# Up projection: product 2 of neighbouring pairs as seven half-size products, and gate sums by an adding DMA

## Chip, cores and metric

The kernel runs on one core of one Trainium2 chip. The metric is the device time of one execution in microseconds (us), as the median of three runs. A profiled execution, recorded by the hardware profiler, is shown beside it.

PE is the matrix engine (TensorE), PEld its weight loads, DVE the vector engine, ACT the scalar engine, POOL the general-purpose engine that also issues DMAs, SP the engine that only issues DMAs. Each engine works through its own queue in order.

## What is computed

Two layers of a hybrid encoder over 1040 frames (16 learned meta frames and 1024 others) of width 1024 in float32. Each layer has attention (not touched here) and a gated feed-forward part:

```python
def conv_ffn(x, w_up, conv_w, conv_b, w_down):
    h = x @ w_up                      # 1024 -> 2 * 2816
    L = h.shape[1]
    hp = jnp.pad(h, ((0, 0), (CONV_W - 1, 0), (0, 0)))
    hc = conv_b
    for j in range(CONV_W):           # causal, width 3
        hc = hc + hp[:, j:j + L] * conv_w[j]
    u, g = jnp.split(hc, 2, axis=-1)
    return (jax.nn.silu(g) * u) @ w_down
```

The change is in `x @ w_up`.

## The kernel before

**Precision.** Every float32 operand is split into two parts, hi (rounded to the matrix engine's format) and lo (the rest). A product is three matmuls: w_hi x_hi, w_lo x_hi and w_hi x_lo (`mm3`, lines 222 to 224). For weights, `up_split` (lines 1067 to 1074) does the split: ACT casts hi (L1072), DVE subtracts to get lo (L1073), both over 128x512 elements (4 k-tiles of 128x128).

**Tiling.** The 5632 output columns are 22 *pairs*: pair j has 128 columns of u and the 128 columns of g that gate them. Channels lie on the 128 partitions, frames along the free dimension, cut into two halves of 520 (layer 0) or 516 and 516 (layer 1), t0 and t1. Within a half, matmuls run over 260 or 258 frames, into two PSUM banks.

**Seven products per pair.** A pair is a 2x2 block product: the block rows are u and g, the inner blocks are channels 0 to 511 and 512 to 1023 (4 k-tiles each), the block columns are the two halves of the frames. It is done in the form of Strassen and Winograd, with seven products p = 1 to 7 instead of eight. The weights are A11, A12 (u, low and high channels), A21, A22 (g) and sums of them: S1 = A21 + A22 (product 5), S2 = S1 - A11 (product 6), A11 - A21 (product 7), A12 - S2 (product 3). Products 1, 2 and 4 use A11, A12 and A22 as they are. The seven moving operands `X[1]` to `X[7]`, each split into hi and lo, are built once per layer (`make_t2` and so on) and stay in SBUF. Product 2 is A12 times `X[2]`, and it goes only into u's half t0.

One product is 4 k-tiles x 2 banks x 3 matmuls = 24 matmuls.

**Order.** `seq` is the order of (pair, product). From pair 5 on it is, for pair j: 2, 6, 5, 7, then product 1 of pair j + 1, then 4, 3. PE's order is fixed by this list; the order of the other engines' queues is laid down by a scheduler when the kernel is built. `ensure(i)` prepares weight operands up to four places ahead (`AHEAD`). hi and lo have three buffers for the even places and three for the odd ones.

**Where weights come from.** `block_operand` (lines 1037 to 1065) loads A11, A21, A22, A12 of a pair by four DMAs from SP when the pair's first product asks for them (L1045), and forms the sums on DVE (`combine`, L1055). A11 and A12 lie in a ring of 4 tiles (tag `raw`), the others in a ring of 7 (`raw2`). For the first five pairs (`N_DMA_SUM`) S1 is not formed on DVE: a DMA loads A21 into a tile (L1048) and a second DMA, from POOL, adds A22 onto it (L1049).

**PSUM.** Four places of two banks each: p0 and p1 alternate by pair for products 1, 6, 7, 4, which add onto one another (bank name a); p2 takes product 5 and then 3 (x); p3 takes product 2 (y, from pair 5 on).

**After each product** (`evacuate`, from line 1260): ACT copies the place of 1, 6, 7, 4 into hu or hg (L1264), DVE adds the others on top (L1263). After product 3 a pair is complete: `conv` (ACT L1252, DVE L1256 twice) for u and for g, SiLU (ACT L1283), the product (DVE L1287), and a store to memory from POOL (L1288).

**Slots.** 33 tiles of 128x1040 float32, and 6 more during the feed-forward part, are lent by `Slots` in the order in which they were given back. The seven moving operands take 4 each, 28 in all. hu, hg and the two results of `conv` take the rest in turn.

**The end of the up projection.** `prepare` is a generator that loads finished pairs back and builds the operands of the down projection, step by step (L337, L1381); `pump` lets it go on when slots are free. `during_last` calls it after each product of the last pair (21), as the moving operands are given back one after another. The down projection then runs first three pairs plainly (288 matmuls), then pairs 3 to 10 as block products, and so on.

## Time and profile before

| | |
|---|---|
| median of 3 runs | 2515.2 us (2514.78 to 2515.3) |
| profiled execution | 2518.04 us, its span 2516.3 us |
| granted clock of PE | 0.996 |
| PE, PEld | 2477.9 us (98%), 2383.8 us (95%), 18442 instructions each |
| DVE | 1767.2 us (70%), 3523 instructions |
| ACT | 1272.9 us (51%), 2733 instructions |
| POOL | 385.3 us (15%), 567 instructions |
| HBM | 177.29 MB read, 67.81 MB written |

The span runs from the first to the last instruction. In layer 0 the up projection lies at about 570 to 1014 us. A row of the timeline reads: start, duration, engine, line, operation, output <- inputs, shapes, count; in brackets, how long the engine was idle before it and what ended that. In a row of the groups by line, the numbers after the bar are busy time in us and the mean of one in ns, then idle time before them and what ended it. Matmul durations overlap; the pace of PE is read from start to start.

### The profile page before, as it was taken

What the parts mean: (1) busy time and instruction counts of PE and PEld (TensorE: products, weight loads), DVE (VectorE), ACT (ScalarE), POOL (GpSimd) and SP (SyncE); (2) the same over time, 40 slices, a digit from 0 to 9 for tenths busy, and PEclk for the clock granted to TensorE, in tenths of its full rate; (3) what the DMA queues carried; (4) which work ended last, traced back from release to release, by engine and by line L of the source; (5) the groups of instructions that cost most, each with busy time, mean ns of one, the idle gap of its engine ahead of it and who ended that gap; (6) DMA issues with size and microseconds to landing.
All of it is one profiled execution on the core that took longest, in us unless ns stands there. A gap on an engine that the chain in (4) does not pass through costs nothing.

```text
span 2516.3 us, 47049 instructions
## 1 busy us (share of the span) xinstructions
PE 2477.9 (98%) x18442; PEld 2383.8 (95%) x18442; DVE 1767.2 (70%) x3523; ACT 1272.9 (51%) x2733; POOL 385.3 (15%) x567
## 2 busy tenths in 40 slices
PE   9999999999999999999999999999999999999998
PEld 8999999999999999999999899999999999997786
DVE  8656777769877777853666666777798777787535
ACT  7346666636544445631443566665464444455312
POOL 2023433210000000100211234331100000001002
PEclk9999999999999999999999999999999999999999
DMA  3232134343322224763312222143433222258722
GB/s 133 67 88 74 44 92 133 118 130 97 119 81 81 77 77 146 193 170 106 107 57 69 74 80 78 58 153 109 142 105 101 76 79 78 80 166 186 194 56 74
DMA packets 118542, 260.94 MB, mean 104 GB/s; under 512 B 14880, under 2 KB 32544, under 8 KB 118320
## 3 DMA queue, kind: packets, MB, share of 16 engines
q1 hardware_dynamic: 93984, 182.79, 23.5%
q0 software_dynamic: 22464, 72.84, 10.4%
q8 instruction: 144, 2.36, 0.4%
q10 hardware_dynamic: 1872, 2.31, 0.3%
q14 instruction: 78, 0.64, 0.1%
HBM read 177.29 MB, written 67.81 MB: 97 GB/s over the span
## 4 chain that ended last, share of the span: by engine, by line
PE 81%; DVE 10%; ACT 4%; DMA 2%; issue 2%; SPq 0%; POOL 0%; DVEq 0%; ACTq 0%; POOLq 0%
PE up L222 11%; PE up L224 11%; PE up L223 11%; PE mm L222 7%; PE mm L224 7%; PE mm L223 7%; PE down L222 5%; PE down L223 5%; PE down L224 5%; PE av L720 3%; PE tr L694 2%; DVE S L661 1%; PE S L658 1%; ACT P L673 1%; PE S L659 1%
## 5 line engine op out<-in xcount | busy, mean ns | idle before, releaser
L222 PE MATMUL up<-x,hi 128*128 128x260 f32 (+1 forms) x2464 | 696.6, 283 | 0.0
L224 PE MATMUL up<-x,hi 128*128 128x260 f32 (+1 forms) x2464 | 695.9, 282 | 0.7 <-DVE x L1097 0.7
L223 PE MATMUL up<-x,lo 128*128 128x260 f32 (+1 forms) x2464 | 696.3, 283 | 0.0
L224 PEld LDWEIGHTS up<-x,hi 128*128 128x128 f32 x2464 | 465.3, 189 | 1.1 <-DVE x L1097 1.1
L222 PEld LDWEIGHTS up<-x,hi 128*128 128x128 f32 x2464 | 464.5, 189 | 0.4 <-DVE hu L1263 0.2
L223 PEld LDWEIGHTS up<-x,lo 128*128 128x128 f32 x2464 | 464.5, 189 | 0.1
L1073 DVE TENSOR_TENSOR lo<-raw,hi 128x512 fp32r<-128x512 f32 x364 | 247.7, 685 | 173.0 <-ACT hi L1072 172.7
L222 PE MATMUL mm<-xh,hi 128*128 128x348 f32 (+4 forms) x1056 | 362.7, 343 | 0.0
L224 PE MATMUL mm<-xl,hi 128*128 128x348 f32 (+4 forms) x1056 | 339.8, 322 | 0.0
L223 PE MATMUL mm<-xh,lo 128*128 128x348 f32 (+4 forms) x1056 | 339.4, 321 | 0.0
L1072 ACT CAST hi<-raw 128x512 fp32r<-128x512 f32 x364 | 223.6, 620 | 128.1 <-PE up L224 84.5
L222 PEld LDWEIGHTS mm<-xh,hi 128*128 128x128 f32 x1056 | 199.5, 189 | 5.2 <-issue 4.6
L223 PEld LDWEIGHTS mm<-xh,lo 128*128 128x128 f32 x1056 | 199.5, 189 | 0.7 <-issue 0.7
L224 PEld LDWEIGHTS mm<-xl,hi 128*128 128x128 f32 x1056 | 198.3, 188 | 0.4 <-issue 0.3
L189 ACT CAST hi<-raw 128x512 fp32r<-128x512 f32 (+2 forms) x168 | 97.4, 581 | 176.0 <-PE down L224 97.0
L223 PE MATMUL down<-ah,lo 128*128 128x260 f32 (+1 forms) x528 | 168.6, 319 | 0.4 <-DVE lo L191 0.3
L224 PE MATMUL down<-al,hi 128*128 128x260 f32 (+1 forms) x528 | 168.5, 319 | 0.0
L222 PE MATMUL down<-ah,hi 128*128 128x260 f32 (+1 forms) x528 | 168.2, 319 | 0.0
L673 ACT ACTIVATE P<-S,m 116x460 f32<-116x460 f32 (+2 forms) x224 | 124.8, 561 | 71.2 <-DVE m L661 67.6
L337 DVE TENSOR_TENSOR PT<-tr,PT 116x464 fp32r<-116x464 f32 (+3 forms) x240 | 122.8, 514 | 46.9 <-ACT PT L336 45.3
L1055 DVE TENSOR_TENSOR raw<-raw,raw 128x512 f32<-128x512 f32 x198 | 129.4, 684 | 17.2 <-DMA raw<-in_wd_dram 16.5
L1288 POOL DMA_DIRECT2D actd<-cv x44 | 23.6, 535 | 756.9 <-DVE cv L1287 735.9
(289 smaller groups left out, 5623.8 us busy)
## 6 DMA issues: line engine op xcount, KB each, us to landing
raw<-in_wm_dram SPq DMA_DIRECT2D x330, 256.0 KB, 2.7
raw<-in_wd_dram SPq DMA_DIRECT2D x64, 256.0 KB, 3.6
actd<-cv POOLq DMA_DIRECT2D x22, 520.0 KB, 3.0
actd<-cv POOLq DMA_DIRECT2D x22, 512.0 KB, 2.9
cb<-cd SPq DMA_DIRECT2D x16, 520.0 KB, 4.1
st<-actd SPq DMA_DIRECT2D x14, 520.0 KB, 4.9
st<-actd SPq DMA_DIRECT2D x14, 512.0 KB, 4.6
kA<-kA SPq DMA_DIRECT2D x24, 260.0 KB, 3.9
```

Of the source, the lines that this page charges most:

```text
L189: nc.scalar.copy(hi[:, :n, :], raw[:, :n, :])
L222: nc.tensor.matmul(ps, wh, xh[:, c0:c0 + n], start=first, stop=False, skip_group_check=more)
L223: nc.tensor.matmul(ps, wl, xh[:, c0:c0 + n], start=False, stop=False, skip_group_check=more)
L224: nc.tensor.matmul(ps, wh, xl[:, c0:c0 + n], start=False, stop=last, skip_group_check=more)
L337: nc.vector.tensor_tensor(out=lo, in0=src, in1=hi.bitcast(F32), op=ALU.subtract)
L658: nc.tensor.matmul(S[:rows, :n], q["qA"][e][:, qs], q["kA"][e][:, c0:k1], start=True, stop=False)
L673: nc.scalar.activation(P[:rows, :n], S[:rows, :n], AF.Exp, scale=-1.0, bias=m[:rows, nch - 1:nch], accum_out=(den if nch == 1 else d3[:row ...
L694: nc.tensor.transpose(tr[:w, 3 - j, :rows], P[:rows, o:o + w], id_)
L720: nc.tensor.matmul(av[:, a:b], w.rearrange("p a b -> p (a b)"), x, start=(t == ts[0] and part == 0 and i == 0), stop=(t == last and i == 1))
L1055: nc.vector.tensor_tensor(out=q[out][:, :nk, :], in0=q[a][:, :nk, :], in1=q[b][:, :nk, :], op=op)
L1072: nc.scalar.copy(hi[:, :nk, :], src[:, :nk, :])
L1073: nc.vector.tensor_tensor(out=lo[:, :nk, :], in0=src[:, :nk, :], in1=hi[:, :nk, :].bitcast(F32), op=ALU.subtract)
```

## The change

Three things.

1. **Pairs 6 to 21, two by two.** Product 2 of pair j and of pair j + 1 (j = 6, 8, ... 20) together are a block product again: the block rows are the two pairs, the inner blocks are the first two and the last two of the four k-tiles, the block columns are the two groups of 260 (258) frames of `X[2]`. They are done as seven half-size products m = 1 to 7, listed in `seq` as (j, SUB + m). Each has 2 k-tiles x 1 bank x 3 matmuls = 6 matmuls. Their weights are made by `sub_operand` from A12 of both pairs; their moving operands are views of `X[2]` for m = 1, 2, 3 and four new tiles `Y[4]` to `Y[7]` (one slot each), built by `second_level` in steps during pairs 4 and 5: two sums (`whole`) of hi and lo of `X[2]`, then for each Y one combination and one split (`make`). Their results go to place p3, one bank for 1, 6, 7, 4 and one for 2, then 5, 3; after each, DVE adds a bank onto a quarter of hu of one of the two pairs (`sub_evacuate`; m = 5 waits until product 1 of pair j + 1 was copied).
2. **S1 by DMA for all pairs.** The DMA that loads A21 and the adding DMA from POOL, for pairs 0 to 4 before, are used for all 22.
3. Product 3's weights A12 - S2 are written over S2, no longer over A12, which the half-size products still need. `X[2]` and `Y` are given back after the last half-size product of pair 20, with a call of `during_last`, and no longer after product 2 of pair 21.

```diff
-N_DMA_SUM = 5
+FIRST_SUB = 6
+SUB = 20
...
@@ up_operand
+        src = lambda j: (self.wm[lyr, M_UP + 2 * j], self.wm[lyr, M_UP + 2 * j + 1], 4, j)
+        if p > SUB:
+            self.block_raws(*src(j), fw, raws, True)
+            self.block_raws(*src(j + 1), fw, raws, only="A12")
+            return self.sub_operand(raws[j], raws[j + 1], p - SUB, fw, odd)
+        return self.block_operand(*src(j), p, fw, raws, odd, True)
+
+    def sub_operand(self, q, r, m, fw, odd):
+        A, B = q["A12"], r["A12"]
+        lo, hi = slice(0, 2), slice(2, 4)
+        tt = lambda out, a, b, op: self.nc.vector.tensor_tensor(out=out, in0=a, in1=b, op=op)
+        if m == 6:
+            q["s"] = fw.tile([128, 4, 128], F32, tag="raw2", name="raw2")
+            tt(q["s"][:, lo, :], B[:, lo, :], B[:, hi, :], ALU.add)
+            tt(q["s"][:, hi, :], q["s"][:, lo, :], A[:, lo, :], ALU.subtract)
+        elif m == 7:
+            tt(q["s"][:, lo, :], A[:, lo, :], B[:, lo, :], ALU.subtract)
+        elif m == 3:
+            tt(q["s"][:, hi, :], A[:, hi, :], q["s"][:, hi, :], ALU.subtract)
+        src, at = {1: (A, lo), 2: (A, hi), 3: (q.get("s"), hi), 4: (B, hi), 5: (q.get("s"), lo),
+                   6: (q.get("s"), hi), 7: (q.get("s"), lo)}[m]
+        return self.up_split(src[:, at, :], fw, odd, 2)
...
@@ block_operand: its loads are now block_raws(u, g, nk, j, fw, raws, by_dma, only)
-            combine("A12", "A12", "S2", ALU.subtract)
+            combine("S2", "A12", "S2", ALU.subtract)
...
@@ ffn_up
-        for j in range(3, NFF - 1):
+        for j in range(3, FIRST_SUB):
             seq += ([(j, 2)] if j > 4 else []) + [(j, 6), (j, 5), (j, 7), (j + 1, 1), (j, 4), (j, 3)]
-        seq += [(NFF - 1, p) for p in (6, 5, 7, 2, 4, 3)]
+        for j in range(FIRST_SUB, NFF, 2):
+            m = lambda i: (j, SUB + i)
+            seq += [m(1), m(2), (j, 6), m(6), (j, 5), m(5), (j, 7), (j + 1, 1), m(7), (j, 4), m(3), (j, 3)]
+            seq += [m(4), (j + 1, 6), (j + 1, 5), (j + 1, 7)] + ([(j + 2, 1)] if j + 2 < NFF else [])
+            seq += [(j + 1, 4), (j + 1, 3)]
...
+        def second_level():
...
+            return [whole(0), whole(1), *make(7, b12, b22, b12, ALU.subtract), *make(6, b11, b12, b11, ALU.add),
+                    *make(5, b22, b22, b11, ALU.subtract), *make(4, b21, b21, b11, ALU.subtract),
+                    lambda: s.put(*t)]
...
+        def sub_evacuate(j, m):
+            bank = sub_bank(m)
+            to, c = {1: (j, 0), 2: (j, 0), 6: (j, 1), 3: (j, 1), 5: (j + 1, 1), 7: (j + 1, 1), 4: (j + 1, 0)}[m]
+            o = st[to]["u"][:, halves[0] + c * n:halves[0] + c * n + n]
+            nc.vector.tensor_tensor(out=o, in0=st[j]["s"][:, bank, :n], in1=o, op=ALU.add)
+        sub_bank = lambda m: 0 if m in (1, 6, 7, 4) else 1
...
+            if p > SUB:
+                m = p - SUB
+                if m == 1:
+                    q["s"] = bank2("sub", 3)
+                xs, c0 = sub_moving(m)
+                first = m in (1, 2, 5)
+                for k in range(2):
+                    self.mm3(q["s"][:, sub_bank(m), :n], ops[i][k], xs[k], c0, n, first and k == 0, k == 1, not first)
+                ops[i] = None
+                evacuate(j, p)
+                if (j, m) == (NFF - 2, 4):
+                    for x in X.pop(2):
+                        s.put(*x)
+                    s.put(*Y.values())
+                    during_last(2)
+                continue
```

More of the change, by code (lines that the diff above doesn't have):

```diff
@@ L1034, in up_operand @@
             return self.up_split(src, fw, odd)
-        return self.block_operand(self.wm[lyr, M_UP + 2 * j], self.wm[lyr, M_UP + 2 * j + 1], 4, j, p, fw, raws, odd, j < N_DMA_SUM)
+        src = lambda j: (self.wm[lyr, M_UP + 2 * j], self.wm[lyr, M_UP + 2 * j + 1], 4, j)
[4 more added lines that the diff above has]
+        return self.block_operand(*src(j), p, fw, raws, odd, True)
@@ new lines, in block_raws @@
+    def block_raws(self, u, g, nk, j, fw, raws, by_dma=False, only=None):
+        nc = self.nc
+        q = raws.setdefault(j, {})
+        for name, src, k0, own in (("A11", u, 0, True), ("A21", g, 0, False), ("A22", g, nk, False), ("A12", u, nk, True)):
+            if name in q or only not in (None, name):
+                continue
+            q[name] = self.wp.tile([128, 4, 128], F32, tag="raw", name="raw", bufs=4) if own else \
+                fw.tile([128, 4, 128], F32, tag="raw2", name="raw2")
+            nc.sync.dma_start(q[name][:, :nk, :], src[:, k0:k0 + nk, :])
+        if by_dma and "S1" not in q:
+            q["S1"] = fw.tile([128, 4, 128], F32, tag="raw2", name="raw2")
+            nc.sync.dma_start(q["S1"][:], g[:, 0:4, :])
+            nc.gpsimd.dma_start(q["S1"][:], g[:, 4:8, :], accum_op=ALU.add)
@@ L1037, in block_operand @@
     def block_operand(self, u, g, nk, j, p, fw, raws, odd, by_dma=False):
         nc = self.nc
-        if j not in raws:
-            q = raws[j] = {}
-            for name, src, k0, own in (("A11", u, 0, True), ("A21", g, 0, False), ("A22", g, nk, False), ("A12", u, nk, True)):
-                q[name] = self.wp.tile([128, 4, 128], F32, tag="raw", name="raw", bufs=4) if own else \
-                    fw.tile([128, 4, 128], F32, tag="raw2", name="raw2")
-                nc.sync.dma_start(q[name][:, :nk, :], src[:, k0:k0 + nk, :])
-            if by_dma:
-                q["S1"] = fw.tile([128, 4, 128], F32, tag="raw2", name="raw2")
-                nc.sync.dma_start(q["S1"][:], g[:, 0:4, :])
-                nc.gpsimd.dma_start(q["S1"][:], g[:, 4:8, :], accum_op=ALU.add)
+        self.block_raws(u, g, nk, j, fw, raws, by_dma)
@@ L1062, in block_operand @@
         elif p == 3:
-            combine("A12", "A12", "S2", ALU.subtract)
-        src = q[{1: "A11", 2: "A12", 3: "A12", 4: "A22", 5: "S1", 6: "S2", 7: "A21"}[p]]
+            combine("S2", "A12", "S2", ALU.subtract)
+        src = q[{1: "A11", 2: "A12", 3: "S2", 4: "A22", 5: "S1", 6: "S2", 7: "A21"}[p]]
         return self.up_split(src, fw, odd, nk)
@@ L1244, in ffn_up @@
         before = {1: second_half, 2: make_t2, 7: make_t3, 8: make_n4, 11: make_t1, 14: make_b22}
-        st = {}
+        st, building = {}, []
         def conv(hb, idx):
@@ L1259, in conv, with whole, make, f @@
             return t
+        Y = {}
+        def second_level():
+            at0, at1 = slice(0, n), slice(n, W)
+            t = [half_slot("t") for _ in range(2)]
+            def whole(i):
+                return lambda: nc.vector.tensor_tensor(out=t[i].t[:, :, :W], in0=X[2][0][i].t[:, :, :W].bitcast(F32),
+                                                       in1=X[2][1][i].t[:, :, :W].bitcast(F32), op=ALU.add)
+            b11, b12, b21, b22 = (x.t[:, :, at] for x in t for at in (at0, at1))
+            def make(m, out, a, b, op):
+                def f():
+                    nc.vector.tensor_tensor(out=out, in0=a, in1=b, op=op)
+                def g():
+                    Y[m] = y = s.get(F32R, f"y{m}", (128, 4, 260))
+                    self.split(y.t[:, 0:2, :n], y.t[:, 2:4, :n], out)
+                return [f, g]
+            return [whole(0), whole(1), *make(7, b12, b22, b12, ALU.subtract), *make(6, b11, b12, b11, ALU.add),
+                    *make(5, b22, b22, b11, ALU.subtract), *make(4, b21, b21, b11, ALU.subtract),
+                    lambda: s.put(*t)]
+        def sub_moving(m):
+            if m in Y:
+                return [(Y[m].t[:, k, :], Y[m].t[:, 2 + k, :]) for k in range(2)], 0
+            i, c0 = {1: (0, 0), 2: (1, 0), 3: (1, n)}[m]
+            return [(X[2][0][i].t[:, k, :], X[2][1][i].t[:, k, :]) for k in range(2)], c0
+        def sub_evacuate(j, m):
[4 more added lines that the diff above has]
+        sub_bank = lambda m: 0 if m in (1, 6, 7, 4) else 1
         def evacuate(j, p):
+            if p > SUB:
+                if p - SUB != 5:
+                    sub_evacuate(j, p - SUB)
+                return
             q = st[j]
@@ L1271, in evacuate @@
                     copy(q["u"][:, t0], bank)
+                if "s" in st.get(j - 1, ()) and p == 1:
+                    sub_evacuate(j - 1, 5)
             elif p == 6:
@@ L1289, in evacuate @@
                 s.put(u, g)
-                del st[j]
+                if "s" not in q:
+                    del st[j]
             q.setdefault("done", set()).add(p)
@@ L1298, in ffn_up @@
                 before[i]()
-            q = st.setdefault(j, {})
+            if (j, p) == (4, 6):
+                building = second_level()
+            if j in (4, 5) and (j, p) != (4, 1) and building:
+                building.pop(0)()
+            if p == SUB + 1:
+                while building:
+                    building.pop(0)()
+            q = st.setdefault(j, {})
+            if p > SUB:
+                m = p - SUB
[12 more added lines that the diff above has]
+                    during_last(2)
+                continue
             bank, first = {2: "y", 5: "x", 3: "x"}.get(p, "a"), p in (1, 2, 5)
```

## The prediction

> **What bounds the kernel now.** I read the page first, then busy time by stage, then the timeline of one pair in the up projection, then the groups by line for prices.

> ```profile
> span 2516.3 us, 47049 instructions
> PE 2477.9 (98%) x18442; PEld 2383.8 (95%) x18442; DVE 1767.2 (70%) x3523; ACT 1272.9 (51%) x2733; POOL 385.3 (15%) x567
> ```

> Busy time by stage (us of the span, then busy time of each engine with its instructions, granted clock, DMA share, GB/s):

> ```profile
> core 0: us, PE busy (x) PEld busy (x) DVE busy (x) ACT busy (x) POOL busy (x), PEclk, DMA share, GB/s
> 620.00:640.00 20.00, 20.00 (x170) 20.00 (x169) 20.00 (x25) 12.66 (x17) 1.91 (x3) 1.00 0.33 117
> 660.00:680.00 20.00, 20.00 (x170) 20.00 (x169) 16.31 (x22) 11.02 (x16) 0.53 (x1) 1.00 0.24 81
> 680.00:700.00 20.00, 20.00 (x169) 20.00 (x169) 14.73 (x20) 9.70 (x14) 0.53 (x1) 1.00 0.24 80
> 700.00:720.00 20.00, 20.00 (x170) 20.00 (x170) 14.73 (x20) 9.70 (x14) 0.53 (x1) 1.00 0.24 80
> 996.00:1044.00 48.00, 47.98 (x402) 47.77 (x401) 47.80 (x50) 34.27 (x47) 6.24 (x8) 1.00 0.74 178
> ```

> PE has no idle time in any up-projection stretch, at full clock. In the steady part (680 to 720) DVE has about a quarter of its time free and ACT half. Twice DVE is full as well: while the first pairs run (620 to 640) and at the end of the up projection (996 to 1044); even there PE does not wait. So a matmul that goes is time saved, as long as DVE does not come late, and the end stretch is where it has least to spare.

> The pace of PE is read from the stores of finished pairs, one per pair, for both layers:

> ```profile
> 723.28 0.53 POOL L1288 DMA_DIRECT2D actd<-cv  x1 [19.53 <-DVE cv L1287]
> 743.35 0.53 POOL L1288 DMA_DIRECT2D actd<-cv  x1 [19.54 <-DVE cv L1287]
> ...
> 2048.56 0.53 POOL L1288 DMA_DIRECT2D actd<-cv  x1 [19.64 <-DVE cv L1287]
> 2068.78 0.53 POOL L1288 DMA_DIRECT2D actd<-cv  x1 [19.69 <-DVE cv L1287]
> ```

> A pair is 7 products of 4 k-tiles, 2 column halves and 3 matmuls: 168 matmuls in 20.07 us in layer 0 (0.1195 us each, 2.87 us per product) and in 20.22 in layer 1 (0.1203).

> **The matmuls.** Two products 2 are 2 x 24 = 48 matmuls; the seven half-size products are 7 x 2 k-tiles x 1 column half x 3 = 42. Six go, for each of the neighbouring pairs that start at 6, 8, ... 20: 8 groups per layer, 48 matmuls per layer. 48 x 0.1195 + 48 x 0.1203 = 5.7 + 5.8 = 11.5 us. The shape of a matmul (128x128 weights, 260 or 258 columns) and one weight load per matmul stay, so the pace should too. [...]

> **DVE and ACT work.** Prices:

> ```profile
> L1073 DVE TENSOR_TENSOR lo<-raw,hi 128x512 fp32r<-128x512 f32 x364 | 247.7, 685 | 173.0 <-ACT hi L1072 172.7
> L1055 DVE TENSOR_TENSOR raw<-raw,raw 128x512 f32<-128x512 f32 x198 | 129.4, 684 | 17.2 <-DMA raw<-in_wd_dram 16.5
> L1263 DVE TENSOR_TENSOR hu<-up,hu 128x520 f32<-128x520 f32 x44 | 30.4, 692 | 0.0
> L1611 DVE TENSOR_TENSOR h<-mm,h 128x256 f32<-128x256 f32 x24 | 9.5, 412 | 2.6 <-PE mm L224 2.6
> ```

> The timeline of DVE at the end of one pair, after its product 3, shows how these follow one another; below it is that of ACT:

> ```profile
> 714.48 1.30 DVE L1256 SCALAR_TENSOR_TENSOR cv<-hg,vec,cv 128x1039 f32<-128x1039 f32 x1 [0.47 <-ACT cv L1252]
> 715.70 0.69 DVE L1263 TENSOR_TENSOR hu<-up,hu 128x520 f32<-128x520 f32 x1
> 716.31 1.29 DVE L1256 SCALAR_TENSOR_TENSOR cv<-hg,vec,cv 128x1038 f32<-128x1038 f32 x1
> 717.52 0.68 DVE L1073 TENSOR_TENSOR lo<-raw,hi 128x512 fp32r<-128x512 f32 x1
> 718.12 1.29 DVE L1256 SCALAR_TENSOR_TENSOR cv<-hu,vec,cv 128x1039 f32<-128x1039 f32 x1
> 719.33 0.69 DVE L1263 TENSOR_TENSOR hu<-up,hu 128x520 f32<-128x520 f32 x1
> 719.94 1.28 DVE L1256 SCALAR_TENSOR_TENSOR cv<-hu,vec,cv 128x1038 f32<-128x1038 f32 x1
> 721.15 0.68 DVE L1073 TENSOR_TENSOR lo<-raw,hi 128x512 fp32r<-128x512 f32 x1
> 721.75 1.23 DVE L1287 TENSOR_TENSOR cv<-cv 128x1040 f32<-128x1040 f32 x1
> ```

> ```profile
> 712.18 0.59 ACT L1264 COPY hg<-up 128x520 f32<-128x520 f32 x1 [1.74 <-PE up L224]
> 712.66 0.62 ACT L1072 CAST hi<-raw 128x512 fp32r<-128x512 f32 x1
> 713.19 1.26 ACT L1252 ACTIVATE cv<-hg,vec 128x1040 f32<-128x1040 f32 x1
> 716.43 1.26 ACT L1252 ACTIVATE cv<-hu,vec 128x1040 f32<-128x1040 f32 x1 [0.78 <-DVE hu L1263]
> ```

> Consecutive DVE instructions overlap by 0.08 us: a 0.68 one takes 0.60 of DVE (717.52 to 718.12), a 1.29 one 1.21. A half-size one, by the 256-column row, takes 0.41 - 0.08 = 0.33. A pair before: 7 splits and 4 sums at 0.60, 3 additions from PSUM at 0.61, 4 convolution steps at 1.21, the gate product 1.15: 14.4 us, as the stretch 700 to 720 shows (14.73 busy).

> Per two pairs the change takes away 2 splits, 2 gate sums and 2 PSUM additions (3.6 us) and adds 7 half splits, 4 half sums and 7 half PSUM additions (18 x 0.33 = 5.9). DVE goes from 28.8 us in 40.1 to 31.1 in 39.4, 79%; not the bound. ACT loses two 0.62 casts and gains seven half ones, at most 7 x 0.62, so under 3.1 us more of its free half. Product 3 of the first level writes its difference to another tile: same size, nothing.

> [...]

> The new moving operands are built once per layer, while pairs 4 and 5 run: 2 sums over 1040 columns (1.15 each, by L1287), 4 combinations and 4 splits at 0.61: 7.2 us. Pairs 4 and 5 lie at about 658 to 695, where DVE has 3.7 + 5.3 us free in 40. It fits, barely; from 620 to 640 DVE had nothing free and PE lost nothing, so I take 0, the end nearest to that row, with the 7.2 us of a layer as the other.

> **The gate sums by DMA.** For 17 more pairs per layer: one more load on SP's queue, and one adding load on POOL's. The ten that exist (duration on POOL, then the times to landing of the adding and of the plain load):

> ```profile
> L1049 POOL DMA_DIRECT2D raw<-in_wm_dram x10: 867/883/917, 559.4 to 1883.3; - x10
> ...
> DMA to landing us min/median/max: 3.9/4.2/4.8
> ...
> DMA to landing us min/median/max: 2.5/3.4/4.2
> ```

> Load, issue and addition make 3.4 + 0.9 + 4.2 = 8.5 us; they are issued with the pair's other weights, four places before its product 1, and its product 6 comes 5 to 7 places after that: at least 15 us. The adding DMA waits on POOL for the load; queued behind it are only stores of finished pairs, for which nobody in the up projection waits. Or it waits behind such a store: 723.28 lies 8.3 us after product 3, and 8.3 + 5.1 us still ends before the next pair's product 6 (two pairs' groups put at least 17 us between). L1055's idle time names only down weights, so sums by DMA did not hold DVE so far. DMA share rises by a quarter of 0.24. I take 0.

> **New waits of PE.** The half-size products share two PSUM banks. The tightest: half product 6 adds onto the bank of half product 1, so DVE must have added product 1 to the pair's tile of hidden values (hu) first. Between lie half product 2 and a full product 6: 0.72 + 2.87 = 3.6 us. This falls right behind the previous pair's product 3, so into the convolution block above. Mapped onto it: the copy at 712.18 follows product 4, product 3 ends at 715.05, half product 1 at 715.8, half product 6 would start at 719.35. At 717.52 DVE did a weight split, because the convolution of hu had to wait for ACT (716.43 + 1.26 = 717.69). The addition is ready at 715.9 and older in the order than most splits; there it ends at 717.95, 1.4 us early. Cost 0 at this place; at the place of the later hu addition (719.33) it ends at 719.75, a 0.4 us stall, 16 x 0.4 = 6.4 us. Operands have six buffers, so one can be built as soon as the operand six places earlier is used; with the half-size ones between, the lead shrinks from 5 x 2.87 = 14.3 us to 7.9 at worst: about as long as the block above (714.48 to 722.9, 8.4 us), which lets splits in at 717.52 and 721.15. Cost 0.

> **The end of the up projection** is where I charge something.

> ```profile
> 1042.22 1.23 DVE L337 TENSOR_TENSOR x<-st,x 128x1040 fp32r<-128x1040 f32 x1
> 1043.38 0.68 DVE L1073 TENSOR_TENSOR lo<-raw,hi 128x512 fp32r<-128x512 f32 x1
> ...
> 1050.78 0.59 ACT L1445 COPY du<-down 128x520 f32<-128x520 f32 x1 [1.22 <-PE down L224]
> ```

> The copy at 1050.78 ends the first block product of the down projection, which thus began at 1047.9. Its operands were ready at 1044.06, behind DVE's full stretch: 3.8 us to spare. In the stretch PE loses a product 2 of pair 21 and gains a half product: 2.15 us shorter. DVE loses a split and an addition and gains a half addition: 0.9 shorter. And there is less room early: of 39 slots the seven moving operands hold 28 and the new ones 4, so at the first release (product 1 of pair 21) 8 are free where 12 were; two or three preparation steps (1.15 each) move later, into the full stretch. 3.8 - 2.15 + 0.9 - 3.4 = -0.9 us. I take a stall of 1.2 us per layer, with 0 and 5.7 (a layer's whole saving) as the ends.

> **Sum.** The profiled execution took 2518.0: 1.7 beside its span, and 2.8 above the median of the runs; I apply the difference to the median. 2515.2 - 11.5 + 2.4 = 2506.1.

> **Rivals.**
> 1. Slower. The addition of half product 1 is queued behind both convolution steps of hu, at 721.15: it ends at 721.6, and PE stalls 2.2 us at each half product 6: 16 x 2.2 = 36, giving 2515 - 11.5 + 36 = 2540. It decides from 0.7 us per group on (11.5/16). For it: DVE's order is fixed ahead, and this block is dense. Against: the gap at 717.52, and the 719.33 row, where an addition of lower urgency got in before the second step.
> 2. No gain. DVE, full at the end stretch, sets when the down blocks start, so all 5.7 us of each layer come back: 2515. For: 47.80 of 48 busy, few slots. Against: 3.8 us to spare, and work that can be reordered.
> 3. In part: the 0.4 us stalls as well, 6.4 us: 2512.5.
> 4. DVE becomes the bound over two pairs. It needs 8.3 us more per group than I count; nothing shows that. Its time would be as in 1.

> **Chances.** Forecast 0.66 (2503.5 to 2509). Rival 2, 0.12. Rival 3, 0.08. Rivals 1 and 4, 0.14. A measurement tells about 0.2%, 5 us, from no change. Faster by more: 0.70 (the forecast and part of rival 3); same 0.16; slower 0.14. The range leaves out rivals 1 and 4 and the far half of rival 2, as well as the worst of building the operands (2 x 7.2 us): 2502.5 to 2514.5. Its lower end is the full saving, 2503.7, less 1.2, the price I charged to a layer's end, which could come out below nothing since the down projection's preparation gets its last slots in a new order.

> **What would show it.** PE x18346, so 96 fewer. Stores of two pairs 39.4 us apart in layer 0 instead of 40.1. No waits of PE for the new additions in the up projection: if rival 1 holds, PE waits for them some 16 times, over 2 us each. DVE 31 us busy per two pairs. A down start that waits for DVE by 1 to 2 us per layer; by over 5, rival 2. Any wait of DVE for weight sums from DMA would prove my queue reasoning wrong.

## Result and profile after

The changed kernel takes 2596.39 us (median of 4 runs, 2595.06 to 2598.91); the kernel before took 2515.25 beside it (2514.78 to 2516.33). The ratio is 1.0324, 95% interval 1.0307 to 1.0340. The prediction, 2506.1 and faster, was wrong by 90 us and in sign.

The page of the kernel after, its head and the first line of the chain that ended last:

```profile
span 2593.3 us, 47512 instructions
...
PE 2491.3 (96%) x18346; PEld 2389.2 (92%) x18346; DVE 1834.2 (71%) x3733; ACT 1305.5 (50%) x2821; POOL 416.3 (16%) x601
...
PE 75%; DVE 13%; ACT 6%; issue 4%; DMA 2%; POOL 0%; SPq 0%; DVEq 0%; ACTq 0%; POOLq 0%
```

The 96 matmuls are gone, but PE idles: 98% busy has become 96% of a longer span. The waits of PE (which line waited for which; us in total, times, longest) name the place at once:

```profile
PE sub L223 <- DVE hu L1328: 56.8, 32, 2.6
PE down L224 <- DVE lo L192: 4.2, 2, 2.2
PE down L223 <- DVE dg L1544: 3.6, 2, 1.9
```

L223 with output `sub` is the first matmul of a half-size product, L1328 the addition of a half-size product to hu. There are 16 groups, so each waits twice. One group in the timeline of PE, and the same stretch in that of DVE:

```profile
783.84 0.28 PE L225 MATMUL sub<-x,hi 128*128 128x260 f32 x1
786.38 0.39 PE L223 MATMUL sub<-x,hi 128*128 128x260 f32 x1 [2.26 <-DVE hu L1328]
...
800.01 0.28 PE L225 MATMUL up<-x,hi 128*128 128x260 f32 x1
801.43 0.39 PE L223 MATMUL sub<-y,hi 128*128 128x260 f32 x1 [1.15 <-DVE hu L1328]
```

```profile
784.09 0.69 DVE L1337 TENSOR_TENSOR hu<-up,hu 128x520 f32<-128x520 f32 x1
784.70 1.29 DVE L1289 SCALAR_TENSOR_TENSOR cv<-hg,vec,cv 128x1038 f32<-128x1038 f32 x1
785.90 0.42 DVE L1328 TENSOR_TENSOR hu<-sub,hu 128x260 f32<-128x260 f32 x1
...
800.95 0.43 DVE L1328 TENSOR_TENSOR hu<-sub,hu 128x260 f32<-128x260 f32 x1 [1.83 <-ACT hu L1338]
```

The matmul at 783.84 is the last of half product 1. Half product 2 follows at once in the order, but starts at 786.38, just after DVE's addition of half product **1** has ended (785.90 + 0.42). The matmul at 800.01 is the last of product 1 of the second pair; half product 7 waits for the addition of half product **5**. In both cases the waiting product writes the *other* bank than the one that DVE reads. Half product 6, which rival 1 feared for, does not wait.

The stores of finished pairs, of which every second one ends a group of two pairs:

```profile
728.15 0.55 POOL L1364 DMA_DIRECT2D actd<-cv  x1 [15.99 <-DVE cv L1363]
...
773.08 0.55 POOL L1364 DMA_DIRECT2D actd<-cv  x1 [16.27 <-DVE cv L1363]
...
816.50 0.55 POOL L1364 DMA_DIRECT2D actd<-cv  x1 [14.59 <-DVE cv L1363]
```

Two pairs take 44.93, then 43.42 us, where 39.4 was predicted and 40.1 was the time before. Between the two values lies the clock. After the 2.28 us wait that ended at 741.44 the matmuls are 0.217 us apart, not 0.12, for one stretch of 3.4 us; a window of 4 us there shows the granted clock:

```profile
741.44 0.58 PE L223 MATMUL sub<-x,hi 128*128 128x260 f32 x1 [2.28 <-DVE hu L1328]
...
742.69 0.42 PE L225 MATMUL sub<-x,hi 128*128 128x260 f32 x1
742.91 0.42 PE L223 MATMUL up<-x,hi 128*128 128x260 f32 x1
...
744.84 0.28 PE L223 MATMUL up<-x,hi 128*128 128x260 f32 x1
744.96 0.28 PE L224 MATMUL up<-x,lo 128*128 128x260 f32 x1
```

```profile
740.00:744.00 4.00, 2.56 (x12) 2.56 (x13) 4.00 (x5) 2.83 (x3) 0.88 (x1) 0.67 0.46 57
```

In the up projections 11 of the 32 waits are followed by such a stretch (9 of the 16 of half product 2, and both of 2.6 us in the last groups), none of the fourteen of 1.15 us.

Length of the stages, first to last matmul of `up` and of `down` in each layer (us):

| kernel | up 0 | up 1 | down 0 | down 1 |
|---|---|---|---|---|
| before | 444.7 | 448.1 | 210.4 | 206.2 |
| after | 482.2 | 485.0 | 212.5 | 207.4 |
| two_tiles | 440.9 | 443.3 | 214.9 | 205.7 |
| two_tiles_later_prep | 440.8 | 442.4 | 210.9 | 206.9 |

The up projections carry 37.5 + 36.9 = 74.4 of the 77.0 us by which the span grew. With the 11.5 us of matmuls that went, 86 us have to be found: 56.8 of waits; 11 slow stretches at about 15 matmuls x 0.1 = 1.5, so 16.5; and 0.25 for each restart (43.42 is 39.48, the two-tile time below, plus 2.26 + 1.15 plus 0.53), so 8. That is 81; two waits of 0.7 for a copy in the last pairs belong to the rest, and some 3 us are not traced.

### The profile page after: what moved, and what is told of

Read it like the earlier page. It is cut to its first block, busy times and chain, and to the rows that moved or that the text cites. A ratio compares the mean times of both kernels' runs of the same rounds, so it can differ in the third digit from the quotient of the medians.

```text
span 2593.3 us, 47512 instructions
## 1 busy us (share of the span) xinstructions
PE 2491.3 (96%) x18346; PEld 2389.2 (92%) x18346; DVE 1834.2 (71%) x3733; ACT 1305.5 (50%) x2821; POOL 416.3 (16%) x601
## 4 chain that ended last, share of the span: by engine, by line
PE 75%; DVE 13%; ACT 6%; issue 4%; DMA 2%; POOL 0%; SPq 0%; DVEq 0%; ACTq 0%; POOLq 0%
PE up L223 8%; PE up L224 8%; PE up L225 8%; PE mm L223 7%; PE mm L224 6%; PE mm L225 6%; PE down L224 5%; PE down L223 5%; PE down L225 5%; PE av L721 3%; PE tr L695 2%; DVE cv L1289 2%; DVE S L662 1%; PE S L659 1%; PE sub L223 1%
## 5 line engine op out<-in xcount | busy, mean ns | idle before, releaser
L223 PE MATMUL up<-x,hi 128*128 128x260 f32 (+1 forms) x2208 | 630.3, 285 | 2.2 <-ACT hg L1338 1.4
L224 PE MATMUL up<-x,lo 128*128 128x260 f32 (+1 forms) x2208 | 629.0, 285 | 1.5 <-DVE lo L1102 1.5
L225 PE MATMUL up<-x,hi 128*128 128x260 f32 (+1 forms) x2208 | 627.8, 284 | 0.3 <-DVE x L1126 0.3
L223 PEld LDWEIGHTS up<-x,hi 128*128 128x128 f32 x2208 | 422.6, 191 | 3.1 <-ACT hg L1338 1.8
L224 PEld LDWEIGHTS up<-x,lo 128*128 128x128 f32 x2208 | 422.3, 191 | 2.0 <-DVE lo L1102 1.9
L225 PEld LDWEIGHTS up<-x,hi 128*128 128x128 f32 x2208 | 422.2, 191 | 0.5 <-DVE x L1126 0.5
L223 PE MATMUL mm<-xh,hi 128*128 128x348 f32 (+4 forms) x1056 | 362.7, 344 | 0.0
L1102 DVE TENSOR_TENSOR lo<-raw,hi 128x512 fp32r<-128x512 f32 (+1 forms) x444 | 269.2, 621 | 104.4 <-ACT hi L1101 102.8
L1101 ACT CAST hi<-raw 128x512 fp32r<-128x512 f32 (+1 forms) x444 | 250.1, 566 | 181.7 <-PE up L225 88.3
L224 PE MATMUL mm<-xh,lo 128*128 128x348 f32 (+4 forms) x1056 | 339.6, 322 | 0.0
L223 PEld LDWEIGHTS mm<-xh,hi 128*128 128x128 f32 x1056 | 199.6, 189 | 5.2 <-issue 4.6
L224 PEld LDWEIGHTS mm<-xh,lo 128*128 128x128 f32 x1056 | 199.5, 189 | 0.7 <-issue 0.7
L224 PE MATMUL down<-ah,lo 128*128 128x260 f32 (+1 forms) x528 | 170.0, 322 | 4.2 <-DVE lo L192 4.2
L223 PE MATMUL down<-ah,hi 128*128 128x260 f32 (+1 forms) x528 | 170.1, 322 | 0.0
L1338 ACT COPY hg<-up 128x520 f32<-128x520 f32 (+1 forms) x88 | 52.1, 592 | 168.4 <-PE up L225 168.4
L1084 DVE TENSOR_TENSOR raw<-raw,raw 128x512 f32<-128x512 f32 x164 | 112.2, 689 | 32.3 <-DMA raw<-in_wd_dram 20.3
```

The lines of the kernel that those rows point to most:

```text
L223: nc.tensor.matmul(ps, wh, xh[:, c0:c0 + n], start=first, stop=False, skip_group_check=more)
L224: nc.tensor.matmul(ps, wl, xh[:, c0:c0 + n], start=False, stop=False, skip_group_check=more)
L225: nc.tensor.matmul(ps, wh, xl[:, c0:c0 + n], start=False, stop=last, skip_group_check=more)
L1084: nc.vector.tensor_tensor(out=q[out][:, :nk, :], in0=q[a][:, :nk, :], in1=q[b][:, :nk, :], op=op)
L1101: nc.scalar.copy(hi[:, :nk, :], src[:, :nk, :])
L1102: nc.vector.tensor_tensor(out=lo[:, :nk, :], in0=src[:, :nk, :], in1=hi[:, :nk, :].bitcast(F32), op=ALU.subtract)
```

## Experiments

**1. Two tiles for the two banks.** Theory T: the wait is the program's. The two banks of p3 are one tile, and a tile is guarded as one, so PE may not write one bank while DVE still has to read the other. In the order of the built program the first matmul of half product 2 does carry a wait for DVE, though it uses nothing that DVE makes or reads there. Here p3 becomes two tiles of one bank, so the wait's reason goes, and nothing else of the change. (`place_tile` returns a `Two` with the tags p3a and p3b for place 3 and the tile of before for the others; where p3 is used whole, its evacuation becomes two instructions.)

```diff
+class Two:
+    def __init__(self, pp, name, tags, pieces=2):
+        self.parts = [pp.tile([128, 512], F32, tag=tag, name=name, bufs=1) for tag in tags[:pieces]]
+    def __getitem__(self, i):
+        return self.parts[i[1]][i[0], i[2]]
...
-        bank2 = lambda name, i: pp.tile([128, 2, 512], F32, tag=f"p{i}", name=name, bufs=1)
+        bank2 = lambda name, i: place_tile(pp, i, name)
```

> The changed kernel, with PSUM place p3 cut into two tiles of one bank each, so that the two chains of half-size products (1, 6, 7, 4 and 2, 5, 3) lie in different tiles; nothing else in the up projection changes (evacuations of p3 elsewhere become two instructions). Theory T, the two banks of one tile are guarded as one, so half product 2 waits for DVE's addition of half product 1 and half product 7 for that of 5: both waits go, PE waits for hu additions under 5 us in all, time 2503 to 2512. Rival L, the additions are late by themselves in the full DVE queue and half product 6 needs the first one anyway: the wait moves to half product 6 and 20 us or more of the 57 stay, time 2530 to 2575. Rival D, the added DVE work and DMA sums are the cost and the waits are only where it shows: 2580 to 2596.

Measured: 2513.78 us, before 2516.90; ratio 0.9989 (0.9980 to 0.9999). The loss is gone and all 32 waits with it. The steady part of the up projection as one window, and three stores of it:

```profile
680.00:960.00 280.00, 280.00 (x2342) 280.00 (x2341) 229.00 (x355) 145.25 (x234) 19.89 (x28) 1.00 0.37 106
```

```profile
741.13 0.55 POOL L1388 DMA_DIRECT2D actd<-cv  x1 [4.35 <-DVE cv L1387]
...
780.62 0.55 POOL L1388 DMA_DIRECT2D actd<-cv  x1 [4.29 <-DVE cv L1387]
...
820.10 0.55 POOL L1388 DMA_DIRECT2D actd<-cv  x1 [3.12 <-DVE cv L1387]
```

PE is busy without a gap at full clock, and two pairs take 39.48 us. That is the step on which the forecast rested. Theory T holds, and the rest of the change does what was predicted of it in that stretch. Why a tile is guarded as one is not shown: the pool of these places is opened with `reuse_waits="tile"`, and no run changes that option. The time is a little above what was expected; where the rest goes is the matter of experiments 4 and 5.

**Control: the kernel before with the same cut** (two tiles, no half-size products), since the cut adds instructions of its own.

> Control: the kernel with two tiles without any half-size product and with the gate sums as in the kernel before; what remains is p3 as two tiles, and product 3's weights written over S2. Both theories on the change: nothing on PE's path, 2514 to 2518. Rival S of the run beside it: 2518 or more.

Measured: 2515.72, before 2517.79; ratio 0.9995 (0.9985 to 1.0004). The cut alone is worth nothing.

**2. Another order instead of another tile.** If a tile is guarded as one, a half product must not follow closely on another of its group. One tile as in the change; half product 2 later (fix_m2), half product 7 later (fix_m7), or all apart (reorder). The order of one group, as far as product 6 of the second pair:

```diff
-  m(1), m(2), (j, 6), m(6), (j, 5), m(5), (j, 7), (j+1, 1), m(7), (j, 4), m(3), (j, 3), m(4), (j+1, 6)
+  fix_m2:  m(1), (j, 6), m(2), (j, 5), m(6), (j, 7), m(5), (j+1, 1), m(7), (j, 4), m(3), (j, 3), m(4), (j+1, 6)
+  fix_m7:  m(1), m(2), (j, 6), m(6), (j, 5), m(5), (j, 7), (j+1, 1), (j, 4), m(3), (j, 3), m(7), (j+1, 6), m(4)
+  reorder: m(1), (j, 6), m(2), (j, 5), m(6), (j, 7), m(5), (j+1, 1), (j, 4), m(3), (j, 3), m(7), (j+1, 6), m(4)
```

> The changed kernel, with only the first half of the order changed: 1, (j,6), 2, (j,5), 6, (j,7), 5, (j+1,1), 7, ... so that half product 7 still follows product 1 of the second pair and thus waits for the addition of 5. Theory T: the 2.3 us waits go and the 1.15 us ones stay, 16 x 1.2 = 19 us over the freed kernel, 2522 to 2530; and if the drops of the granted clock follow the long waits only, the clock stays at 0.99 or above in every stretch of the up projection. Rival L: as in the changed kernel less what the new order hides, 2540 to 2575. Rival D: 2580 to 2596.

> The changed kernel, one tile, with only the second half of the order changed: half product 7 after product 3 of the first pair, 4 after product 6 of the second; half product 2 still right behind 1. The long stall stays, the short one goes or shrinks. Theory T with a clock that drops after some of the long stalls only: two pairs take 42 to 44 us, about 1.5 us more where the granted clock drops, and drops remain; 2560 to 2580. If instead the drops follow from the number of stalls, they become rarer by half.

> The changed kernel, one tile as it is, but the order of products so that a full product lies between any two half-size ones: 1, (j,6), 2, (j,5), 6, (j,7), 5, (j+1,1), (j,4), 3, (j,3), 7, (j+1,6), 4. Theory T: every wait that the shared tile makes has 2.9 us of PE work to hide it, time 2503 to 2514. Rival L: additions that come over 2.9 us late still stop PE; the first one comes 2.3 us after its product in the changed kernel, so even then under 2530. Rival D: stays at 2580 to 2596.

Measured: fix_m2 2552.39 (ratio 1.0140, 1.0125 to 1.0155), fix_m7 2585.02 (1.0268, 1.0254 to 1.0282), reorder 2560.72 (1.0174, 1.0159 to 1.0189). All three missed, on the slow side. The waits of PE in fix_m7, then in reorder; the timeline of PE in fix_m2:

```profile
PE sub L223 <- DVE hu L1328: 35.7, 16, 2.3
PE down L223 <- DVE h L1633: 8.9, 2, 5.3
PE down L224 <- DVE lo L192: 7.8, 6, 2.1
```

```profile
PE sub L223 <- DVE hu L1328: 19.4, 22, 3.1
...
PE sub L223 <- ACT hi L1101: 4.1, 8, 0.5
```

```profile
785.81 0.36 PE L223 MATMUL sub<-y,hi 128*128 128x260 f32 x1 [0.53 <-DVE hu L1328]
...
794.38 0.39 PE L223 MATMUL sub<-y,hi 128*128 128x260 f32 x1 [1.14 <-DVE hu L1328]
```

Each edit removes the wait that it aimed at. In fix_m2 the 2.26 us of half product 2 are gone, the 1.14 of half product 7 stay, and half product 6 now waits 0.53 for the addition of half product 2, again of the other bank. In fix_m7 those of half product 7 are gone and the sixteen of half product 2 stay; its down stages are 219.3 and 219.2 us long, 9 and 13 us over those of before, which the expectation did not have (DVE is late there, last two lines of the first block). In reorder, 22 waits for other additions and 8 that the profile puts down to a weight operand take the place of the 32, and its down stages are long too (215.1 and 217.0 us). So none of these three orders frees the one tile. A full product, 2.9 us, lies between half products 2 and 6 in fix_m2, but DVE's addition comes later still: half product 2 ends at 782.41 and its addition at 785.66, 3.25 us later. That additions can be more than 2.9 us late is rival L's point; with two tiles, in the order of the change, additions on the same queue cost PE no wait.

**3. The gate sums by DMA.** Alone, on the kernel before; and taken back (but for the first five pairs) in the two-tile version:

```diff
-N_DMA_SUM = 5
+N_DMA_SUM = NFF
```

```diff
-            self.block_raws(*src(j), fw, raws, True)
+            self.block_raws(*src(j), fw, raws, j < 5)
```

> The kernel before, with the gate sums by DMA for all 22 pairs and no half-size products. Theory T and rival L: nothing on PE's path, 2513 to 2517. Rival D: the sums by DMA hold DVE or POOL, over 2525.

> The kernel with two tiles, but the gate sums by DMA for the first five pairs only, as before, and on DVE for the others. By my DVE budget 32.3 us of 39.4 per two pairs: DVE still is not the bound, the up projection stays at 39.4 us per two pairs, and at the end DVE has at most two sums more: 2513 to 2518. Rival D, DVE has no room for the half-size work without the sums by DMA: PE waits for DVE in the up projection, over 2525.

Measured: 2520.83, ratio 1.0012 (1.0002 to 1.0021), slightly slower, above theory T's range and below rival D's; and 2514.37, ratio 0.9987 (0.9978 to 0.9996), the same as the two-tile version with all sums by DMA. So the sums are not the 81 us and not the missing rest. But the waits of DVE in dma_sums_only have a row that the kernel before does not have, and in each layer PE loses one wait to it (at 662.62 and at 1908.92, 2.01 us):

```profile
DVE raw L1055 <- DMA raw<-in_wm_dram: 67.2, 45, 4.8
```

```profile
662.62 0.39 PE L222 MATMUL up<-x,hi 128*128 128x260 f32 x1 [1.85 <-DVE hu L1263]
```

In the two-tile version the same wait adds up to 31.6 us in 23 times, 28.1 of them behind the adding DMA (14 times); PE does not feel it. Not all of it is the price of the sums: with the sums back on DVE, 14 waits for the plain loads remain, 20.7 us.

One of the 14 in the two-tile version, from the load of A21 over the adding DMA to the sum S2 on DVE that uses it, and the row of SP's waits for such loads:

```profile
705.54 0.33 SPq L1094 DMA_DIRECT2D raw<-in_wm_dram  x1
...
710.24 0.87 POOL L1095 DMA_DIRECT2D raw<-in_wm_dram  x1 [8.05 <-ACT hi L1123]
...
714.26 0.69 DVE L1106 TENSOR_TENSOR raw<-raw,raw 128x512 f32<-128x512 f32 x1 [2.27 <-DMA raw<-in_wm_dram]
```

```profile
SPq L1094 <- DVE lo L1124: 142.9, 34, 10.3
```

From the load to the sum it is 8.7 us, as long as the prediction reckoned (8.5). But the load leaves only 6.5 us before DVE is ready for the sum, not 15: SP waits with it, by its waits row, until DVE has split an earlier weight tile. That it waits for that tile's place in the ring of 7 is how I read this row; no run with a longer ring shows it.

**4. Without the last group.** Theory E: what the two-tile version lacks (3.1 of 11.5 us gained) is lost where the up projection ends. Its stores agree: pair 19's lies 6.1 us earlier than before (978.04 against 984.15), pair 21's only 2.6 (1020.69 against 1023.27), and then comes this wait, with the clock low behind it:

```profile
1023.44 0.39 PE L246 MATMUL down<-ah,lo 128*128 128x260 f32 x1 [2.26 <-DVE lo L214]
```

```profile
1020.00:1040.00 20.00, 17.74 (x135) 17.54 (x135) 19.35 (x22) 13.94 (x24) 4.70 (x6) 0.91 0.89 196
```

PE waits for the low part of the weights of the fourth plain down block, behind preparation work on a full DVE. Here pairs 20 and 21 are done as before, seven groups in each layer:

```diff
-        for j in range(FIRST_SUB, NFF, 2):
+        for j in range(FIRST_SUB, NFF - 2, 2):
...
+        j = NFF - 2
+        seq += [(j, 2), (j, 6), (j, 5), (j, 7), (j + 1, 1), (j, 4), (j, 3)]
+        seq += [(NFF - 1, p) for p in (6, 5, 7, 2, 4, 3)]
```

> The kernel with two tiles, but pairs 20 and 21 as in the kernel before, each with a full product 2; seven groups per layer instead of eight. Theory E, what the kernel with two tiles still loses (8 us of the 11.5) is lost at the end of the up projection, where DVE is full and the last group adds work and takes slots: 7 x 6 x 2 matmuls are 10.0 us saved, the stalls of 2.3 and 1.4 us in front of the plain down products and the 0.7 us ones before them go, 2505 to 2509. Rival S, the loss lies in the split evacuations of place p3 or is spread over the up projection: 2514 to 2517.

Measured: 2517.74, before 2517.79; ratio 1.0002 (0.9993 to 1.0011). Missed: the saving is gone altogether. The stall moved, it did not go, in the profiled execution:

```profile
959.47 0.36 PE L245 MATMUL up<-x,hi 128*128 128x260 f32 x1 [1.16 <-DVE hu L1363]
...
2267.79 0.50 PE L246 MATMUL down<-ah,lo 128*128 128x512 f32 x1 [3.04 <-DVE lo L214]
```

The first sits where the last group now ends; the second is the wait for the low part, longer than the two-tile version's 1.42 in layer 1 (0.60 in layer 0). The up projections are only 1.7 and 3.7 us shorter than before, where 5 each were expected; the wait shown and the one of 0.48 us behind it are part of that, the rest was not traced.

**5. Easing the start of the down projection.** Two ways to have that low part earlier, each in the two-tile version and in the kernel before: form it on GpSimd (pool_low; `low` is GpSimd for the eight plain blocks of the first three pairs), or put off three preparation steps (later_prep).

```diff
-            eng = nc.gpsimd if self.att and not self.mixing else nc.vector
+            eng = low or (nc.gpsimd if self.att and not self.mixing else nc.vector)
...
```

```diff
-                self.pump(2)
+                self.pump({0: 0, 1: 1, 4: 3, 5: 3, 6: 3}.get(m, 2) if kind == "n" else 2)
```

> The version with two tiles, and the low parts of the weights of the first three down row blocks (the 128x384 subtractions, 0.55 us each on VectorE, 8 in each layer) formed by GpSimd instead of VectorE. Theory E2 (what the two-tile version lacks of its 11.5 us is mostly one stall at the start of the down projection: 2.26 us at 1023.44 and 1.42 us at 2270.71, each a wait for such a low part behind other work on VectorE, and after the first one a lower granted clock, together 4 to 4.5 us in the first layer and 1.4 us in the second): both stalls go, the down stage of the first layer is as long as before the change (210 us instead of 215), and the time is 0.9955 to 0.9975 of the kernel before, near 2507 to 2511. Rival: VectorE as a whole is late there, and the stall only moves to the next operand that it forms, or GpSimd, whose queue also holds a store that waits for VectorE, is as late (a 128x512 subtraction took it 1.30 us, so a 128x384 one about 1 us): 0.998 to 1.000, as with two tiles alone (0.9989).

> The kernel before, with the low parts of the weights of the first three down row blocks formed by GpSimd, and nothing else changed. It tells whether that step is worth something without the half-size products. There the wait for a low part was 0.33 us in the second layer and below 0.3 us in the first. Theory E2: nothing that can be measured, 0.9985 to 1.0005. Rival: the step is a gain of its own, through less work on VectorE in a stretch that it fills (39.89 of 40 us): below 0.998.

> The version with two tiles, and of the operands of the half-size down products two steps less are formed after the first of the eight plain down blocks and one less after the second, and one more after each of the fifth to the seventh. The low part of the fourth block's weights, for which the two-tile version waited 2.26 us at 1023.44 and 1.42 us at 2270.71, so stands four VectorE operations of 1.23 us earlier in VectorE's order. Theory E2 (that wait, and the lower granted clock after the first of the two, 15 matmuls 0.217 us apart instead of 0.119, 1.5 us, are most of what the two-tile version lacks of its 11.5 us): both waits go, the down stage of the first layer is 210 to 211 us instead of 215, and the time is 0.9960 to 0.9978 of the kernel before, near 2507 to 2511. Rival: VectorE as a whole is late in that stretch, and the stall moves to an operand of the half-size down products (a wait of PE for an x by VectorE near 1045 to 1065): 0.9980 to 1.0000, as with two tiles alone (0.9989).

> The kernel before with the same shift of two steps, and nothing else. It tells whether the shift is worth something without the half-size products. The waits that it could remove are 0.33 us in the second layer and below 0.3 us in the first. Theory E2: nothing that can be measured, 0.9990 to 1.0007. Rival: a gain of its own: below 0.9985.

| | with two tiles | in the kernel before |
|---|---|---|
| pool_low | 2535.38, ratio 1.0074 (1.0061 to 1.0087) | 2525.90, 1.0038 (1.0025 to 1.0051) |
| later_prep | 2514.16, 0.9985 (0.9976 to 0.9994) | 2528.26, 1.0039 (1.0026 to 1.0051) |

pool_low was slower than either theory allowed, in both kernels. Timelines of POOL, DVE and PE with two tiles:

```profile
998.85 9.18 POOL L214 TENSOR_TENSOR lo<-raw,hi 128x384 fp32r<-128x384 f32 x2 [18.42 <-ACT hi L212]
1007.98 0.56 POOL L1388 DMA_DIRECT2D actd<-cv  x1
```

```profile
1008.57 2.12 DVE L1505 TENSOR_TENSOR t<-st 128x1040 f32<-128x1040 f32 x1
1016.77 1.24 DVE L1505 TENSOR_TENSOR st<-st 128x1040 f32<-128x1040 f32 x1 [6.07 <-DMA st<-actd]
```

```profile
1018.67 0.58 PE L245 MATMUL down<-ah,hi 128*128 128x260 f32 x1 [4.40 <-DVE hu L1360]
```

Two subtractions took GpSimd 9.18 us. A store of a finished pair was queued behind them; its load back came late, DVE waited 6.07 us for it, and PE 4.40 for DVE. In layer 1 a single subtraction took 11.31 us, and PE waited for the low part itself:

```profile
2284.18 11.31 POOL L214 TENSOR_TENSOR lo<-raw,hi 128x384 fp32r<-128x384 f32 x1
...
2295.55 0.80 PE L246 MATMUL down<-ah,lo 128*128 128x512 f32 x1 [7.86 <-POOL lo L214]
```

In the kernel before, too, PE waited for such a low part, 3.55 us at 1030.70, behind a subtraction of 6.97 us. So pool_low says nothing on theory E2.

later_prep did what it was meant to: no wait for a low part is left, and the first layer's down stage is 210.9 us instead of 214.9. But at the block products PE now waits for ACT to copy a place out:

```profile
2292.96 0.50 PE L245 MATMUL down<-x,hi 128*128 128x512 f32 x1 [1.75 <-ACT du L1570]
```

There are three such waits (1.08 at 1050.84; 1.75 and 1.37 in layer 1; the two-tile version has one, of 1.15), and the whole is not distinguishable from the two-tile version: 0.9985 lies in the rival's range, though the stall is a copy by ACT and not an operand by VectorE. In the kernel before, the same shift was expected to be worth nothing; it costs some 10 us, with a new wait of 2.69 us at 1055.56 and a down stage of 217.3 us instead of 210.4. So the order in that stretch is balanced to a few us. E2 is not shown: the waits that it named are gone, but the median did not move. The profiled execution of later_prep is the fastest of its eleven (2510.73; median 2514.16), so its stages in the table above are better than typical.

## Why the prediction was wrong

- **The step that failed is "New waits of PE ... Cost 0".** It looked for the matmul that next writes a bank, and found half product 6, 3.6 us behind. What PE waits for is the tile, and the next to write the tile is half product 2, at once. Its timing came out: the addition of half product 1 was placed 2.9 us after the end of product 3 (717.95 against 715.05), and it ends 2.9 us after it (786.32, against a last matmul at 783.12 + 0.28). With 0.7 us to the waiting product instead of 3.6, the same working would have given the 2.2 us wait.
- **A second wait was not on the list**: half product 7 behind that of 5, 1.15 us. The prediction had m = 5 wait for the copy of product 1, and did not ask who then follows 5.
- **Rival 1** had the right kind (a stall per group behind an addition) and one right figure (2.2 us), with the wrong place and the wrong cause. Its 36 us are what the waits of half product 2 cost; those of half product 7 (21 us), the clock and the restarts are the other 50 of the 86.
- **No price for the clock.** It was 1.00 in all stretches read, so a wait was priced at its length. The 1.5 us behind 11 of them are 16 us. The profile before had such cases outside these stretches: after a wait of 2.74 us that ended at 2373.21, the 512-column matmuls lie 0.43 us apart instead of 0.23 for some 3 us, at a granted clock of 0.50.
- **The matmuls**: 39.48 against 40.13 us for two pairs, 0.65 saved of 0.72. Right.
- **DVE**: predicted 79% of the steady part, measured 229.00 of 280 with two tiles, 82%. Not the bound; right.
- **The sums by DMA**: with two tiles the cost of 0 held (ratio 0.9989 with them, 0.9987 without); alone in the kernel before they cost 0.1%. The queue reasoning did not hold. By the prediction's own test ("any wait of DVE for weight sums from DMA") it was wrong: 28.1 us of such waits with two tiles. The time from load to sum was right; the lead of at least 15 us was not, since the load itself leaves late (experiment 3).
- **The end of the up projection**: priced at 1.2 us per layer, on the block products' operands. With two tiles the wait is at another operand, the fourth plain block's low part: 2.26 us and 1.5 of low clock in layer 0, 1.42 in layer 1, besides 0.68 in each for a copy. So 4.4 and 2.1 us by these rows, though no run shows that they set the median (experiment 5): the working followed DVE's queue to the block products and skipped the plain blocks ahead of them. Of the 11.5 us the two-tile version keeps 8.5 in the up projections (3.7 + 4.8; the copy waits and 0.07 per group are most of the difference) and gives 4.0 back in the down stages: 4.5 lost in layer 0, 0.5 gained in layer 1. Of the 4.5, 1.5 are a second low-clock stretch, behind a wait of 2.35 us at 1126.73; the kernel before waited 1.95 there without one. That leaves 4.5, about what its span says (2511.6 against 2516.3); the medians differ by 3.1.

## What to carry to other kernels

When two accumulations share a PSUM tile, ask who writes the *tile* next, not who writes the bank: banks that are filled and drained in turn want tiles of their own (here 56.8 us of waits with one tile, none with two). Where PE is the bound, price a wait at more than its length: here 0.25 us for the restart and, behind 11 of the 18 waits of over 2 us, 1.5 us for a stretch at a granted clock of 0.50. Where a stretch is full on two engines, relief for one operand can show up as a wait for the next (here 1.42 us for a low part went and 1.75 for a copy came); measure it in the kernel it is meant for.

## Hardware behaviour that was not expected

**GpSimd beside a busy VectorE.** Two 128x384 subtractions on GpSimd took 9.18 us from 998.85 on, while VectorE worked without a gap on operations with two inputs until 1005.7. The third, at 1008.56, took 1.02, and there VectorE's 128x1040 operation (1008.57) took 2.12 instead of 1.23: the first time GpSimd was the slow one, here VectorE. The subtraction of 11.31 us in layer 1 (experiment 5) began at 2284.18 and ended at 2295.49; from 2284.35 to 2294.64 VectorE ran nine operations with two inputs in a row, 1.14 us from start to start, and GpSimd ended 0.85 us after the last of them. What slows the one engine beside the other, no run shows.
